# Layer 0's FFN of a two-layer encoder: background transfers issued by GpSimd, and layer 1's Fourier and recurrence input weights split there and loaded as pairs

## The chip, the cores and the metric

The kernel runs on one core of one Trainium2 chip. The metric is the device time of one execution in microseconds; the time of the kernel before is the median of three runs. One further execution was recorded by the hardware profiler, and all rows below come from it. The engines are PE (matrix products), DVE, ACT and POOL (GpSimd); SP only issues transfers here. Every engine works through its own instructions in order, and waits where one of them has to wait. A transfer issued by SP, ACT or POOL stands in that engine's order like any other instruction.

## The reference

Two layers, each with a mixing step and an FFN, on one sequence of 1024 positions and 1024 channels. Everything is float32.

```python
for l in range(DEPTH):
    mod = c_act @ w_ada[l] + b_ada[l]                  # 6 vectors of 1024: shift, scale, gate, twice
    sh1, sc1, gt1, sh2, sc2, gt2 = jnp.split(mod, N_MOD, axis=-1)
    h = modulate(rms_norm(x, g_mix[l]), sh1, sc1)
    p = h @ w_in[l]                                    # Fourier 256, recurrence 384, its gate 384, q, k, v
    y_f = fourier_mix(p_f, w_fourier[l])
    ...                                                # linear recurrence, neighbourhood attention
    y = jnp.concatenate([y_f, y_l, y_n], axis=-1) @ w_out[l]
    x = x + gt1[:, None, :] * y
    h = modulate(rms_norm(x, g_ffn[l]), sh2, sc2)
    f = (jax.nn.silu(h @ w_ffn_gate[l]) * (h @ w_ffn_up[l])) @ w_ffn_down[l]
    x = x + gt2[:, None, :] * f
return rms_norm(x, g_final)
```

## The kernel before

**Products in three parts.** PE multiplies rounded numbers. To come near float32, each operand is split into a rounded part, hi, and the rest, lo, and a product is three matmuls (hi hi, hi lo, lo hi). `split` makes the two: ACT rounds a raw tile into hi (line 199), DVE subtracts hi from it into lo (line 202). So a weight tile costs a load by SP, an ACT pass and a DVE pass before PE (line 191) can use it. In the traces the large tile of raw numbers is called plain, that of split numbers rounded, and U is 1024 columns, HALF 512.

**The FFN of a layer.** The hidden width is cut into slices f of 128. For every f seven P jobs of 12 matmuls each make the gate and up products of that slice (`P_ORDER`); their product is evacuated by ACT and DVE, split, and kept in a tile A: ffa_A for even f, ffb_A for odd f. Beside it lies the slice of down weights (ffa_DW, ffb_DW). In an even f the down products of the two slices before it are made: `down_pair` adds 12 matmuls and one DVE operation (line 205) at eight of the 14 hooks of that f (`PAIRS`). So the work repeats every two f's, 264 matmuls, and the down products of a pair can't start before the second half of its ffb_A is split. From f = 2 on this is one loop, in layer 0 from about 605 to 1185 us, in layer 1 from about 1702 to 2305.

**Background work in layer 0's FFN.** At each hook from f = 3 on, `bg` pulls one or two steps from a generator: first `half_steps`, the product of c with w_ada of layer 1, then `split_spill`. `half_steps` takes w_ada in 96 halves of 256 KB: SP loads one into a raw buffer (line 1527), and DVE multiplies it with c and adds up along the row, in one instruction, a matvec (line 1529), with a small one behind it that reads the sum. `split_spill` takes weights that layer 1 will want, 13 items in 26 pieces: SP loads a piece into the same raw buffer (line 255), ACT and DVE split it, SP stores hi and lo into a DRAM tensor, wspill (line 261). SP also loads the FFN's own weights (lines 1306 and 1457), in the order in which the code is written. There is one raw buffer and one buffer each for hi and lo (M0).

**Layer 1's start.** After the last P job of layer 0 come the last down products, the norm of layer 1 and the input projection, one tile of 128 columns a job. Its first nine loads (tiles T_F, T_F + 1, T_X, T_X + 1 for either half of the positions, then T_X + 2) go by `w_load`: SP loads, ACT and DVE split. The tiles from T_G on, the DFT matrices and wv go by `ready_load`: two loads of POOL's queue (lines 242 and 243) fetch hi and lo from wspill into one of three slots (WX: ready_WR and two slots of rounded). The squares of the norm at lines 380 and following run on ACT, DVE and POOL.

The core of what the change touches, as it stands before:

```python
for j in range(8):
    for i in range(2):
        self.nc.sync.dma_start(out=raw, in_=self.I["ada"][l, 8 * c + j, :, i * HALF:i * HALF + HALF])
        yield 1
        self.nc.vector.tensor_tensor_reduce(out=raw, in0=raw, in1=self.f(self.M0 + i * HALF, HALF), ...)
        yield 1
```

The order on ACT, DVE and PE in the FFN is that of the code: a hook issues its splits, its down pair and then its background steps.

## Time and profile before

| | us |
|---|---|
| median of three runs | 2347.38 (2344.06 to 2350.89) |
| the profiled execution | 2345.14 |
| its span in the trace | 2343.4 |
| PE busy | 2219.9 (95%) |
| DVE busy | 1750.5 (75%) |
| ACT busy | 964.2 (41%) |
| POOL busy | 377.8 (16%) |
| layer 0's FFN loop | about 605 to 1185 |
| layer 1's start | about 1185 to 1262 |
| layer 1's FFN loop | about 1702 to 2305 |

The span runs from the first to the last instruction in the trace; the execution is 1.74 us longer. A share of busy time is a mean over stages: PE is not short of work in the loops, so the places to look at are those where it stands, what it stands for, and what that waits for in turn. The granted clock of PE (PEclk) is given as a share of its full 2.4 GHz; 0.50 is the lower of its two levels, and a window that holds both has a value between. Line numbers are those of the kernel before; in the changed kernel the matvec is line 1532, its load 1528, the spill's load 251 and its store 255.

### The profile page before, as it was taken

Reading aid. Unit: us, or ns where it says so; the run is one execution under the profiler, and the core shown is the slowest. Engines: PE = TensorE matmul, PEld = TensorE weight load, DVE = VectorE, ACT = ScalarE, POOL = GpSimd, SP = SyncE. Lnnn points to the kernel's source line nnn. Section 1 sums busy time; section 2 is a strip of 40 time slices with the busy share of each in tenths; the row PEclk is TensorE's granted clock in tenths of the full one; section 3 lists DMA queues with packets and bytes.
Section 4 is the critical chain, followed back from the end, with each engine's and each line's share of the span. In section 5 each row is a group of like instructions: output and inputs, shape, how many; then the busy total and the mean of one; then the engine's idle time right before and its main releaser. Section 6 shows DMA issues by size and latency. Waiting matters only on the chain.

```text
span 2343.4 us, 27097 instructions
## 1 busy us (share of the span) xinstructions
PE 2219.9 (95%) x9802; PEld 1786.6 (76%) x9802; DVE 1750.5 (75%) x2840; ACT 964.2 (41%) x1608; POOL 377.8 (16%) x302
## 2 busy tenths in 40 slices
PE   6987998999999999999999999899999999999997
PEld 4765876778888887787777787678788888888886
DVE  8888689788788888776676456887876666666666
ACT  5365476444222222333244746745532222222223
POOL 4224276300000000000001445740000000000002
PEclk9997999989999999999999999999999999999998
DMA  8323423331333344465232262323021111111112
GB/s 299 103 67 111 133 82 121 109 118 46 102 121 115 121 124 121 135 201 171 66 133 76 69 195 69 106 80 113 28 63 54 55 54 54 55 52 48 55 37 77
DMA packets 91100, 230.53 MB, mean 98 GB/s; under 512 B 10451, under 2 KB 16083, under 8 KB 90966
## 3 DMA queue, kind: packets, MB, share of 16 engines
q1 hardware_dynamic: 82324, 194.42, 25.9%
q10 hardware_dynamic: 3746, 18.66, 2.3%
q0 software_dynamic: 4896, 15.73, 2.2%
q8 instruction: 77, 1.26, 0.2%
q14 instruction: 57, 0.47, 0.1%
HBM read 207.80 MB, written 20.97 MB: 98 GB/s over the span
## 4 chain that ended last, share of the span: by engine, by line
PE 64%; DVE 21%; DMA 7%; ACT 4%; issue 4%; POOL 1%; SPq 0%; ACTq 0%; DVEq 0%; POOLq 0%
PE psum L191 64%; DVE rounded L202 4%; DVE plain L202 3%; DMA plain<-in_ada 3%; DVE plain L205 2%; ACT plain L199 1%; DMA plain<-in_dft 1%; DVE plain L1529 1%; DVE psum L923 1%; DMA plain<-in_wv 1%; DVE psum L202 1%; DVE rounded L205 1%; DVE plain L341 1%; ACT lru_LF L199 1%; DVE lru_LF L725 1%
## 5 line engine op out<-in xcount | busy, mean ns | idle before, releaser
L191 PE MATMUL psum<-rounded 128*128 128x512 f32 (+2 forms) x4116 | 994.9, 391 | 20.8 <-DVE rounded L209 7.7
L191 PEld LDWEIGHTS psum<-rounded 128*128 128x128 f32 (+1 forms) x4116 | 771.5, 190 | 189.4 <-DVE rounded L209 11.5
L199 ACT ACTIVATE rounded<-plain 128x512 fp32r<-128x512 f32 (+4 forms) x404 | 263.8, 659 | 619.3 <-PE psum L191 472.1
L202 DVE TENSOR_TENSOR rounded<-plain,rounded 128x512 fp32r<-128x512 f32 (+4 forms) x410 | 317.8, 781 | 73.3 <-ACT rounded L199 70.1
L191 PE MATMUL psum<-hx_HX,rounded 128*128 128x512 f32 x1488 | 365.1, 392 | 1.9 <-DVE plain L202 1.9
L205 DVE SCALAR_TENSOR_TENSOR plain<-psum,plain 128x1024 f32<-128x1024 f32 (+2 forms) x256 | 269.9, 1062 | 111.5 <-PE psum L191 109.7
L191 PEld LDWEIGHTS psum<-hx_HX,rounded 128*128 128x128 f32 x1488 | 279.3, 188 | 63.9 <-ACT rounded L199 2.3
L191 PE MATMUL psum<-ffa_A,ffa_DW 128*128 128x512 f32 (+1 forms) x1080 | 299.8, 388 | 0.7 <-ACT plain L199 0.7
L191 PE MATMUL psum<-ffb_A,ffb_DW 128*128 128x512 f32 x960 | 275.0, 393 | 7.6 <-DVE ffb_A L202 4.3
L202 DVE TENSOR_TENSOR plain<-plain 128x512 f32<-128x512 f32 (+4 forms) x342 | 207.2, 617 | 73.1 <-DMA plain<-in_wu 41.2
L380 POOL TENSOR_TENSOR plain<-plain 128x512 f32<-128x512 f32 x6 | 8.1, 1357 | 1459.4 <-ACT plain L199 1459.4
L191 PEld LDWEIGHTS psum<-ffa_A,ffa_DW 128*128 128x128 f32 x1080 | 201.0, 188 | 43.9 <-ACT plain L199 1.5
L202 DVE TENSOR_TENSOR plain<-psum,plain 128x512 f32<-128x512 f32 (+1 forms) x288 | 193.4, 685 | 46.3 <-PE psum L191 42.5
L191 PEld LDWEIGHTS psum<-ffb_A,ffb_DW 128*128 128x128 f32 x960 | 179.7, 188 | 52.5 <-DVE ffb_A L202 8.6
L199 ACT ACTIVATE plain<-plain 128x512 f32<-128x512 f32 (+6 forms) x191 | 117.8, 629 | 152.2 <-DVE plain L202 76.7
L960 POOL TENSOR_TENSOR rounded<-qk_PE,rounded 128x512 fp32r<-128x512 f32 (+3 forms) x132 | 141.2, 1077 | 131.8 <-ACT rounded L199 107.6
L191 PE MATMUL psum<-rounded,v_V 128*65 128x512 f32 (+4 forms) x528 | 128.3, 357 | 14.5 <-ACT rounded L199 4.9
L191 PE MATMUL psum<-qk_QT 128*128 128x512 f32 (+8 forms) x432 | 107.7, 349 | 20.5 <-DVE plain L923 14.3
L191 PEld LDWEIGHTS psum<-rounded,v_V 128*65 128x65 f32 (+1 forms) x528 | 74.0, 149 | 52.2 <-POOL rounded L960 6.3
L202 DVE TENSOR_TENSOR psum<-psum,plain 128x256 f32<-128x256 f32 x240 | 97.7, 410 | 21.0 <-PE psum L191 14.3
L199 ACT ACTIVATE qk_PE<-psum 128x512 f32<-128x512 f32 (+4 forms) x168 | 83.4, 503 | 55.7 <-DVE psum L202 50.3
L199 ACT ACTIVATE ffa_DW<-plain 128x512 fp32r<-128x512 f32 x44 | 27.8, 631 | 186.0 <-PE psum L191 184.1
(140 smaller groups left out, 2138.2 us busy)
## 6 DMA issues: line engine op xcount, KB each, us to landing
plain<-in_ada SPq DMA_DIRECT2D x96, 256.0 KB, 2.6
plain<-in_wd SPq DMA_DIRECT2D x88, 256.0 KB, 2.6
plain<-in_wg SPq DMA_DIRECT2D x40, 512.0 KB, 3.6
plain<-in_wu SPq DMA_DIRECT2D x40, 512.0 KB, 3.6
plain<-in_ada SPq DMA_DIRECT2D x30, 512.0 KB, 3.5
wspill<-plain SPq DMA_DIRECT2D x44, 256.0 KB, 2.9
start_AT<-in_ada SPq DMA_DIRECT2D x18, 512.0 KB, 5.1
plain<-in_bias_t ACTq DMA_DIRECT2D x12, 768.0 KB, 4.6
```

The lines of the kernel that those rows point to most:

```text
L191: self.nc.tensor.matmul(out=out, lhsT=lhsT, rhs=rhs, start=start, stop=stop)
L199: self.nc.scalar.activation(out=out, in_=in_, func=func, **kw)
L202: self.nc.vector.tensor_tensor(out=out, in0=a, in1=b, op=op)
L205: self.nc.vector.scalar_tensor_tensor(out=out, in0=a, scalar=s, in1=b, op0=op0, op1=op1)
L341: self.nc.vector.tensor_tensor_reduce(out=raw, in0=raw, in1=self.f(self.M0, U), op0=ALU.mult, op1=ALU.add, scale=1.0, scalar=0.0, accum_ou ...
L380: (self.nc.gpsimd if eng[m] else self.nc.vector).tensor_tensor(out=accs[i], in0=accs[i], in1=ss[i], op=ALU.add)
L725: nc.vector.tensor_tensor_scan(out=t, data0=a, data1=i, initial=0.0, op0=ALU.mult, op1=ALU.add)
L923: self.nc.vector.tensor_tensor_reduce(out=s, in0=s, in1=self.f(bo, a * w).rearrange("p (a b) -> p a b", a=a), op0=ALU.add, op1=ALU.max, sc ...
L960: (self.nc.vector if PLAN[self.l]["lo"][self.step] else self.nc.gpsimd).tensor_tensor(out=pl, in0=p, in1=ph.bitcast(F32), op=ALU.subtract)
L1529: self.nc.vector.tensor_tensor_reduce(out=raw, in0=raw, in1=self.f(self.M0 + i * HALF, HALF), op0=ALU.mult, op1=ALU.add, scale=1.0, scalar ...
```

## The change

The loads of `half_steps` move from SP's queue to POOL's. They use two raw buffers in turn, the old one and `r2`, which is taken from the FFN's list of free temporaries (four stay in it instead of five). A step now issues the load of one half and the matvec of the half before: 97 steps instead of 192.

`split_spill` moves to POOL's queue as well. It loads into the two raw buffers in turn, splits the piece before, and stores hi and lo by one transfer out of one pair buffer in M0. A piece takes two steps instead of three. Five items come in (T_F, T_F + 1, T_X, T_X + 1, T_X + 2 of layer 1): 18 items, 36 pieces.

`ready_load` fetches hi and lo by one transfer of 1 MB instead of two of 512 KB; the slots (WX) are set at the last P job of layer 0's FFN, first two of rounded, later three. All jobs of layer 1's input projection take their weights this way. `bg` is called with one step at every hook. Steps in all: 171 instead of 270.

```diff
     def ready_load(self, i, n):
         def go():
-            hi, lo = [a[:, :n] for a in self.WX()]
-            self.nc.gpsimd.dma_start(out=hi, in_=self.ws[i, :, 0, :n])
-            self.nc.gpsimd.dma_start(out=lo, in_=self.ws[i, :, 1, :n])
-            return hi, lo
+            w = self.WX().rearrange("p (t n) -> p t n", t=2)[:, :, :n]
+            self.nc.gpsimd.dma_start(out=w, in_=self.ws[i, :, :, :n])
+            return w[:, 0], w[:, 1]
         return go
 
     def split_spill(self):
-        raw = self.f(10 * U + HALF, HALF)
-        for i, (w, n) in enumerate(src):
-            for c in range(0, n, HALF):
-                m = min(HALF, n - c)
-                self.nc.sync.dma_start(out=raw[:, :m], in_=w[:, c:c + m])
-                yield 1
-                hi, lo = [self.f(o, m).bitcast(F32R) for o in h]
-                self.split(raw[:, :m], hi, lo)
-                yield 1
-                for j, a in enumerate((hi, lo)):
-                    self.nc.sync.dma_start(out=self.ws[i, :, j, c:c + m], in_=a.bitcast(F32))
-                yield 1
+        q, h = self.nc.gpsimd, self.f(self.M0, U).bitcast(F32R).rearrange("p (t n) -> p t n", t=2)
+        pieces = [(i, w, c, min(HALF, n - c)) for i, (w, n) in enumerate(self.spilled()) for c in range(0, n, HALF)]
+        for j, (i, w, c, m) in enumerate(pieces + [(0, None, 0, 0)]):
+            if w is not None:
+                q.dma_start(out=self.raw2(j)[:, :m], in_=w[:, c:c + m])
+            if j:
+                i, w, c, m = pieces[j - 1]
+                self.split(self.raw2(j - 1)[:, :m], h[:, 0, :m], h[:, 1, :m])
+                q.dma_start(out=self.ws[i, :, :, c:c + m], in_=h[:, :, :m].bitcast(F32))
+            yield 1
+            yield 1
...
+    SPILL = (T_G, T_G + 1, T_G + 2, T_K, T_Q, T_F, T_F + 1, T_X, T_X + 1, T_X + 2)
...
+    def raw2(self, j):
+        return self.f((10 * U + HALF, self.r2)[j % 2], HALF)
...
-        i = {T_G: 0, T_G + 1: 1, T_G + 2: 2, T_K: 3, T_Q: 4}.get(t) if l else None
-        if i is not None:
-            return self.ready_load(i, U), fn, True
+        if l:
+            return self.ready_load(self.SPILL.index(t), U), fn, True
...
-            self.WX = Ring([slot(self.WR1, 0), slot(self.RA, 16 * U), slot(self.RA, 18 * U)])
+            self.WX = Ring([self.WR1, *self.WX.items[::-1]])
...
             if l == 0 and f == FIRST + 1 and i == 0:
+                self.r2 = self.free.pop()
...
-            self.bg(1 if f % 2 or i < 3 or i > 10 else 2)
+            self.bg(1)
 
     def half_steps(self, seq):
+        halves = [(l, c, j, i) for l, c in seq for j in range(8) for i in range(2)]
+        for q, (l, c, j, i) in enumerate(halves + [(0, 0, 0, 0)]):
+            if q < len(halves):
+                self.nc.gpsimd.dma_start(out=self.raw2(q), in_=self.I["ada"][l, 8 * c + j, :, i * HALF:i * HALF + HALF])
+            if q:
+                l, c, j, i = halves[q - 1]
+                part, raw = [self.mod[l] + 8 * c, self.tiny], self.raw2(q - 1)
+                self.nc.vector.tensor_tensor_reduce(
...
+            yield 1
...
                 self.WH, self.WS = Ring([o, 34 * U - o]), U
+                self.WX = Ring([self.RA[:, a:a + 2 * U] for a in (o, 34 * U - o)])
```

**The order on DVE.** First the middle of layer 0's FFN, at the down weights of the second pair of f's. The rows named ISA are the matvec (128x512) and the reading of its sum (128x1); a wait named DMAHW is on a transfer of SP's or ACT's queue, DMASW on one of POOL's. Before:

```order
L202 TENSOR_TENSOR rounded<-plain,rounded 128x512 [waits PE_49,Activation_49]
L205 SCALAR_TENSOR_TENSOR plain<-plain 128x8 [waits DVE_49]
L202 TENSOR_TENSOR plain<-psum,plain 128x512 [waits PE_49]
L1529 ISA plain<-plain 128x512 [waits DMAHW0_49]
L1529 ISA plain 128x1
L202 TENSOR_TENSOR plain<-psum,plain 128x512 [waits DVE_49]
L202 TENSOR_TENSOR rounded<-plain,rounded 128x512 [waits Activation_49]
```

After, on DVE at the same down weights:

```order
L1532 ISA plain<-plain 128x512 [waits DMASW2_49]
L1532 ISA plain 128x1
L1532 ISA plain<-plain 128x512 [waits DMASW3_49]
L1532 ISA plain 128x1
L202 TENSOR_TENSOR plain<-psum,plain 128x512 [waits PE_49]
L202 TENSOR_TENSOR rounded<-plain,rounded 128x512 [waits DMAHW2_49,Activation_49]
L202 TENSOR_TENSOR plain<-plain 128x512 [waits DMAHW3_49]
L205 SCALAR_TENSOR_TENSOR plain<-psum,plain 128x1024 [waits PE_49]
L1532 ISA plain<-plain 128x512 [waits DMASW4_49]
```

One matvec between some six other operations has become two side by side, every four or so.

**The order on ACT.** The end of a pair of f's during the spill, where the two halves of ffb_A are rounded. A row plain<-plain that waits for a DMA is the rounding of a piece of the spill into M0. Before, on ACT:

```order
L199 ACTIVATE plain<-plain 128x512 [waits DMAHW5_49,DMAHW3_49,Activation_49]
L199 ACTIVATE rounded<-plain 128x512 [waits DVE_49,PE_49]
L199 ACTIVATE plain<-plain 128x512 [waits DVE_49]
L199 ACTIVATE plain<-plain 128x512 [waits DMAHW7_49,DMAHW1_49,Activation_49]
L199 ACTIVATE rounded<-plain 128x512 [waits DVE_49,PE_49]
L199 ACTIVATE rounded<-plain 128x512 [waits PE_49]
L199 ACTIVATE ffb_A_3674<-plain 128x512 [waits DVE_49]
```

After, on ACT at the end of a pair of f's, each spill rounding waiting for its own load and for the store of the piece before:

```order
L199 ACTIVATE plain<-plain 128x256 [waits DMASW2_49,DMASW1_49,Activation_49]
L199 ACTIVATE plain<-plain 128x512 [waits DVE_49]
L199 ACTIVATE rounded<-plain 128x512 [waits DVE_49,PE_49]
L199 ACTIVATE ffb_A_3674<-plain 128x512 [waits DVE_49]
L199 ACTIVATE plain<-plain 128x512 [waits DMASW4_49,DMASW3_49,Activation_49]
L199 ACTIVATE rounded<-plain 128x512 [waits PE_49]
L199 ACTIVATE rounded<-plain 128x512 [waits DMAHW1_49,PE_49]
L199 ACTIVATE ffb_A_3674<-plain 128x512 [waits DVE_49]
```

A rounding of the spill now stands between the two halves of ffb_A as well, and its two waits are both for POOL's transfers.

**The order on POOL.** The change of layers: squares of layer 1's norm (plain<-plain) and the loads from wspill. Before:

```order
L380 TENSOR_TENSOR plain<-plain 128x512 [waits DMAHW2_49,DMAHW1_49,DMAHW3_49,PE_49,DMAHW5_49,Activation_49,Pool_49]
L380 TENSOR_TENSOR plain<-plain 128x512 [waits Activation_49] x2
L242 DMA ready_WR_8026<-wspill 128x1024 [waits DMAHW2_49,DMAHW6_49,DVE_49,PE_49]
L243 DMA ready_WR_8026<-wspill 128x1024 [waits DMAHW7_49,DMAHW4_49]
L242 DMA rounded<-wspill 128x1024 [waits DMAHW1_49,DMAHW5_49,DVE_49,PE_49]
L243 DMA rounded<-wspill 128x1024 [waits DMAHW6_49,DMAHW2_49,PE_49]
```

After, on POOL, from the last stores of the spill on:

```order
L255 DMA wspill<-plain 256x1x512 [waits DMASW6_49,DVE_49]
L255 DMA wspill<-plain 256x1x256 [waits DVE_49]
L242 DMA rounded<-wspill 128x2048 [waits DMASW0_49,DVE_49,PE_49]
L242 DMA rounded<-wspill 128x2048 [waits DVE_49,PE_49]
L384 TENSOR_TENSOR plain<-plain 128x512 [waits DMASW5_49,Activation_49,Pool_49]
L384 TENSOR_TENSOR plain<-plain 128x512 [waits Activation_49] x2
L242 DMA ready_WR_8022<-wspill 128x2048 [waits DMASW2_49,DVE_49,PE_49]
```

Two loads of whole pairs have moved ahead of the squares, and each load from wspill is one row where there were two.

## Rows read from the trace of the kernel before

**Rows 1.** The page, part 1: busy us, share of the span, instructions.

```profile
PE 2219.9 (95%) x9802; PEld 1786.6 (76%) x9802; DVE 1750.5 (75%) x2840; ACT 964.2 (41%) x1608; POOL 377.8 (16%) x302
```

**Rows 2.** The chain that ended last, by time: start us, us, what.

```profile
610.24 0.70 DVE plain L1529 x2
...
619.01 2.40 DVE plain L202 x4
626.90 30.06 PE psum L191 x130
...
687.91 30.03 PE psum L191 x130
...
854.52 0.71 DVE plain L1529 x2
855.24 2.63 DMA plain<-in_ada
...
870.97 30.03 PE psum L191 x130
...
995.18 30.02 PE psum L191 x130
...
1034.10 0.70 DVE plain L202
1035.20 3.94 DMA plain<-in_dft
...
1121.90 62.02 PE psum L191 x263
...
1701.05 602.59 PE psum L191 x2633
```

**Rows 3.** Waits of PE, 605 to 1185: us in total, times, longest.

```profile
PE psum L191 <- DVE ffb_A L202: 3.3, 7, 0.7
PE psum L191 <- ACT ffb_A L199: 3.2, 3, 2.2
```

**Rows 4.** Busy time by window: us, PE, PEld, DVE, ACT, POOL, granted clock, DMA share, GB/s.

```profile
1120.76:1124.20 3.44, 2.79 (x7) 2.02 (x8) 1.69 (x3) 0.61 (x1) 0.00 (x0) 0.71 0.47 157
...
1216.27:1219.70 3.43, 3.43 (x18) 3.14 (x19) 0.87 (x2) 0.27 (x1) 0.00 (x0) 0.72 0.47 158
```

**Rows 5.** PE's timeline after 1121.90: start us, us, engine, line, operation, tiles, count.

```profile
1122.70 1.48 PE L191 MATMUL psum<-ffa_A,ffa_DW 128*128 128x512 f32 x3
...
1126.81 0.85 PE L191 MATMUL psum<-ffa_A,ffa_DW 128*128 128x512 f32 x3
```

**Rows 6.** Line 1529, the matvec: ns min/median/max; idle of DVE ahead of it (us, times).

```profile
L1529 DVE CUSTOM_DVE_ANT_0 plain<-plain x96: 677/684/696, 610.2 to 972.9; 128x512 f32<-128x512 f32 x96
...
  DMA plain<-in_ada: 26.5, 37
```

**Rows 7.** DMA issues on SP: count, KB each, median us from issue to landing.

```profile
plain<-in_ada SPq DMA_DIRECT2D x96, 256.0 KB, 2.6
...
plain<-in_wg SPq DMA_DIRECT2D x40, 512.0 KB, 3.6
...
xspill<-plain SPq DMA_DIRECT2D x8, 512.0 KB, 2.9
```

**Rows 8.** Line 242, POOL's load of hi from wspill (512 or 384 KB).

```profile
DMA to landing us min/median/max: 3.9/4.3/5.3
```

**Rows 9.** Line 255, SP's loads of the spill's pieces.

```profile
DMA to landing us min/median/max: 2.6/3.7/4.7
```

**Rows 10.** PE's timeline at layer 1's start.

```profile
1216.27 1.82 PE L191 MATMUL psum<-plain 128*128 128x1 f32 x14 [1.28 <-DVE plain L380]
```

**Rows 11.** DVE's timeline there.

```profile
1214.38 1.23 DVE L202 TENSOR_TENSOR rounded<-plain,rounded 128x1024 fp32r<-128x1024 f32 x1 [0.43 <-ACT rounded L199]
```

**Rows 12.** Line 243, POOL's load of lo, issued behind that of hi.

```profile
DMA to landing us min/median/max: 4.2/4.9/7.2
```

**Rows 13.** POOL's timeline: the first load into rounded.

```profile
1258.10 0.53 POOL L242 DMA_DIRECT2D rounded<-wspill  x1 [53.67 <-PE psum L191]
```

More of the change, by code (lines that the diff above doesn't have):

```diff
@@ L137, in __init__ @@
         self.xs = dr.tile([8, P, S], F32, name="xspill")
-        self.ws = dr.tile([13, P, 2, U], F32, name="wspill")
+        self.ws = dr.tile([18, P, 2, U], F32, name="wspill")
         self.X0 = 0
@@ L240, in go, with spilled @@
         def go():
[L241 to L244 removed]
+            w = self.WX().rearrange("p (t n) -> p t n", t=2)[:, :, :n]
+            self.nc.gpsimd.dma_start(out=w, in_=self.ws[i, :, :, :n])
+            return w[:, 0], w[:, 1]
         return go
     def split_spill(self):
[L248 to L262 removed]
+        q, h = self.nc.gpsimd, self.f(self.M0, U).bitcast(F32R).rearrange("p (t n) -> p t n", t=2)
[10 more added lines that the diff above has]
+    SPILL = (T_G, T_G + 1, T_G + 2, T_K, T_Q, T_F, T_F + 1, T_X, T_X + 1, T_X + 2)
+    def spilled(self):
+        src = [(self.I["w_in"][1, t], U) for t in self.SPILL]
+        return src + [(self.I["dft"][c], U) for c in range(4)] + [(self.I["wv"][1, k], 768) for k in range(4)]
+    def raw2(self, j):
+        return self.f((10 * U + HALF, self.r2)[j % 2], HALF)
     def pull(self):
@@ L1087, in mix @@
             wx = self.open("ready", WR1=(2 * U, F32R))
-            slot = lambda a, o: (a[:, o:o + U], a[:, o + U:o + 2 * U])
-            self.WX = Ring([slot(self.WR1, 0), slot(self.RA, 16 * U), slot(self.RA, 18 * U)])
+            self.WX = Ring([self.WR1, *self.WX.items[::-1]])
             self.deep = 2
@@ L1518, in hook @@
                 self.c_spread()
-            self.bg(1 if f % 2 or i < 3 or i > 10 else 2)
+            self.bg(1)
     def half_steps(self, seq):
-        raw = self.f(10 * U + HALF, HALF)
-        for l, c in seq:
-            part = [self.mod[l] + 8 * c, self.tiny]
-            for j in range(8):
-                for i in range(2):
-                    self.nc.sync.dma_start(out=raw, in_=self.I["ada"][l, 8 * c + j, :, i * HALF:i * HALF + HALF])
-                    yield 1
-                    self.nc.vector.tensor_tensor_reduce(
-                        out=raw, in0=raw, in1=self.f(self.M0 + i * HALF, HALF), op0=ALU.mult, op1=ALU.add,
-                        scale=1.0, scalar=0.0, accum_out=self.f(part[i] + j, 1))
-                    yield 1
-            m = self.f(part[0], 8)
-            self.tt(m, m, self.v(l, V_ADA + 8 * c, 8), ALU.add)
-            self.tt(m, m, self.f(self.tiny, 8), ALU.add)
+        halves = [(l, c, j, i) for l, c in seq for j in range(8) for i in range(2)]
[6 more added lines that the diff above has]
+                self.nc.vector.tensor_tensor_reduce(
+                    out=raw, in0=raw, in1=self.f(self.M0 + i * HALF, HALF), op0=ALU.mult, op1=ALU.add,
+                    scale=1.0, scalar=0.0, accum_out=self.f(part[i] + j, 1))
+                if (j, i) == (7, 1):
+                    m = self.f(part[0], 8)
+                    self.tt(m, m, self.v(l, V_ADA + 8 * c, 8), ALU.add)
+                    self.tt(m, m, self.f(self.tiny, 8), ALU.add)
+            yield 1
     def ffn_jobs(self, l):
```

7 lines of the change are left out of this document (2 added, 5 removed).

## The prediction

> **What bounds the kernel now.** The page's first part comes first: TensorE (PE) is busy 95% of the span, DVE 75%, ACT 41% [rows 1], so the question is where PE is not. The chain of waits [rows 2] shows where. Layer 1's FFN is one unbroken piece of PE work, 2633 matmuls in 602.59 us, 0.229 us a matmul. In layer 0's FFN the same work is broken at even distances: a pair of f's is 264 matmuls, 60.42 us at that rate, and the pieces begin later and later against it. From 626.90 to 870.97 lie four pairs, 244.07 us against 241.68: 2.4 lost. From 870.97 to 1121.90 lie four more, 250.93 us: 9.25 lost. Between the pieces the chain names matvecs and in_ada loads in the first stretch, in_dft and other loads of the spill in the second. PE's table of waits for the stage [rows 3] has the end of it: 6.5 us in ten waits for ffb_A tiles. After the longest of them the granted clock is 0.71 [rows 4]; three matmuls there take 1.48 us, three at full clock 0.85 [rows 5]. Eight ran so, at about 0.43 instead of 0.23: 1.6 us. So this FFN holds 2.4 + 9.25 + 1.6 = **13.3 us** that can be won, and none of it is PE's own work.
>
> Why ffb_A is late is read off DVE. It works in order, and each of the 96 matvecs (0.684 us, [rows 6]) stands in its row between the splits that PE needs. 37 times DVE idled until an in_ada load landed, 26.5 us in all. Load and matvec share one buffer: a load is issued when the matvec before it ends, and DVE stands until it has landed. The spill has the same form, a chain of load, ACT rounding, DVE subtraction, next load. 22 of its 26 loads are issued between 995.18 and 1121.90 [rows 2]: 126.72/22 = 5.76 us each, 11 a pair, 63.4 us where PE wants 60.42. That is the 3 us a pair that the second stretch loses.
>
> **The change, part by part.** (1) *ada halves on GpSimd's queue, two buffers.* The matvecs now stand in pairs (first order excerpt), 28 to a pair of f's. The work is the same 96; what decides is the cycle of the two buffers, from one pair of matvecs to the next: c = 0.71 + 0.01 + L + 0.03, the first two from the matvec at 854.52 and the load issued behind it at 855.24 [rows 2], the last an allowance for the semaphore. L, a 256 KB load issued by GpSimd, is in no row. On SP that load lands in 2.6, one of 512 KB in 3.6 [rows 7]; on GpSimd 512 KB takes 4.3 [rows 8]. So the ends are 2.6 and 4.3, and I take 2.6 + (4.3 - 3.6) = **3.3**, GpSimd's surcharge at equal size added to SP's row of the same size, the nearest. c = 4.05.
>
> A pair of matvecs can't start before the first, at 610.24 [rows 2], plus its cycles. By the new order 10 matvecs stand ahead of the second ffb_A of the first pair of f's, 41 ahead of the next one, 69 and 96 ahead of the others. First: 610.2 + 4c + 3.7 (a matvec and five operations of 0.60 behind it, as in the four at 619.01) = 630.1, against 626.90: 3.2 late. Second: 610.2 + 20c + 1.9 = 693.1 against 687.91 [rows 2]: **5.2** late. Third: 610.2 + 34c + 1.9 = 749.8, before the 753.5 that PE reaches a pair after the second, so nothing is added. Twenty cycles make it steep: L = 3.1 gives 1.2, 3.65 gives 12, 2.6 nothing, and L = 4.3 (c = 5.05) holds every later pair of f's to 14c = 70.7, some 43 over the stage.
>
> The Trainium skill, page "DMA: Bandwidth & Descriptors", section "Anatomy of one DMA — SWDGE (gpsimd) path", gives a fixed 2.0 us and the bytes at 436 GB/s for such a transfer: an estimate of 2.6 for 256 KB, 3.2 for 512 KB. The row of 512 KB has 4.3 [rows 8], so the trace speaks against that price; by the page's figure the ada halves would cost PE nothing. Its section "Issuing engine by pattern" names Sync for plain loads, which speaks against this move.
>
> (2) *The spill.* 18 items in 36 pieces instead of 13 in 26, on GpSimd, loads double-buffered, but one buffer for hi and lo. The chain is now ACT rounding, DVE subtraction, store's landing, next rounding: the rounding waits for the store before it (second excerpt), and ACT, in order, holds the ffb_A rounding behind it. Before, 5.76 less the load's 3.7 [rows 9] leaves 2.06 for ACT, DVE and what lies between; 0.4 of it is the two stores' own issue ahead of the next load (1034.10 + 0.70 to 1035.20, [rows 2]). So a cycle is 1.66 + L. L, a 512 KB store by GpSimd: at least 2.9, SP's xspill store of that size [rows 7], at most 4.3 [rows 8]; I take 2.9 + 0.7 = 3.6, by the same surcharge. A cycle is 5.26. ACT's new order holds 10 pieces in the first pair of f's, 12 in each of the next two: 12 x 5.26 = 63.1, 2.7 over, twice, of which ACT's look-ahead over PE hides a little: **4**. It decides from 60.42/12 = 5.03. At L = 2.9 it costs nothing; at 4.3 it is 12 x 5.96 = 71.5, 11.1 over, 22 in all. The ten added pieces' roundings and subtractions are hidden: ACT and DVE have the room [rows 1].
>
> (3) *SP loses 96 ada loads and the spill.* Weight loads no longer queue behind an SP that waits for a matvec: part of the 13.3, nothing on top. One step a hook instead of one or two: 171 steps instead of 270, which end in time either way. If they did not, the rest would stand in the open ahead of the last down projections.
>
> (4) *Layer 1's start.* The w_in tiles of Fourier and recurrence inputs come split: nine SP loads, nine ACT roundings and nine DVE subtractions go. On the path stands one: PE waited 1.28 at 1216.27 [rows 10] for DVE, which had a subtraction of 1.23 at 1214.38 just ahead [rows 11]; then the granted clock is 0.72 [rows 4], another 1.6. Removed: 2.9; late next is the square itself, which then ends about when PE comes. Added: one load of 1 MB in place of two of 512 KB. The second landed 4.9 after its issue [rows 12], issued behind the first one's 0.53 [rows 13]: about 5.5. A half job is 24 matmuls, 24 x 0.229 = 5.5. Where a single slot turns over, the load just fills the job, so I put 0.5, from 0 to +4 if each of five such jobs waits 0.8. Sum **-2.4** (-2.9 to +1.1). The squares on GpSimd stand behind two of these loads (third excerpt); those wait for a slot that the last P jobs no longer read, so they cost two issues of 0.53 before the squares' inputs exist.
>
> **Sum.** -13.3 + 5.2 + 4 + 1.5 (a few waits like those of [rows 3] that stay) - 2.4 = -5.0 on a span of 2343.4: 2338.4, and 1.74 around it (2345.14 profiled): 2340.1. The profiled execution lies 2.24 under the median 2347.38, so the median should be **2342**.
>
> **Rivals.** *A, the forecast*: 2342, 0.42. *B, GpSimd's transfers are as quick as SP's*: neither cycle reaches PE, -13.3 + 1.5 - 2.4 = -14.2, 2333. For it: GpSimd's engine has nothing else to do in this stage, and the 4.3 was measured with two loads in flight. Against: that row lies 0.7 over SP's. 0.25. The page's price named above points the same way. *C, the store's landing paces ACT*: the single hi/lo buffer makes each rounding wait for it; at 4.3 two pairs of f's take 71.5, 18 more than in A, +13.0: 2360, slower. It passes the time before from a cycle of 5.5. For it: the second of two GpSimd transfers took 4.9 [rows 12]. Against: SP's stores land sooner than its loads of that size [rows 7]. 0.18. *D, the ada loads pace DVE at 4.3*: +43 instead of +5.2: 2380; it needs a half-size load to take what a full one does. 0.07. *E, it doesn't do what it says*: ffb_A is late by DVE's order, not by the transfers, and only layer 1's start is won: 2345. DVE's 26.5 us idle for the loads [rows 6] and the chain's DMAs [rows 2] speak against. 0.08.
>
> **Numbers.** A measurement tells about 0.3%, 7 us, from no change: faster is under 2340.3, slower over 2354.4. A lies at 2335 to 2349 by its bounds: 0.14 under, 0.27 within, 0.01 above. B: 0.24 faster, 0.01 within. C: 0.16 slower, 0.02 within. D: slower. E: within. Together 0.38, 0.38, 0.24. The range of 8 in 10 takes A, B, E and the lower half of C: 2331 to 2361.
>
> **What would show it.** Loads of in_ada by GpSimd landing in 3.1 to 3.5; two matvecs every 4.05 in the first pair of f's; PE waiting for ffb_A some 3 us near 630 and 2 more near 690, then hardly until the spill; stores of wspill landing near 3.6 with ACT idle until they do, and pairs of 61 to 63 us from 930 on; no split ahead of PE near 1216. B shows as PE work that runs on from pair to pair; C as ACT's table of waits led by wspill stores. The forecast falls if the loads land outside 2.9 to 3.7, or if the spill's cycle passes 5.5.

## The result, and the profile after

| | before | after |
|---|---|---|
| median, us | 2348.56 (4 runs) | 2379.78 (2377.9 to 2382.98, 4 runs) |
| profiled execution / span, us | 2345.14 / 2343.4 | 2382.98 / 2381.1 |

The changed kernel is 1.4% slower: the ratio is 1.0138, with a 95% interval from 1.0121 to 1.0155. The forecast was 2342 in a range from 2331 to 2361, so it has the wrong sign and the time is outside the range.

Both programs have the same 9802 matmuls in the same order, so they can be laid side by side: how much later does the same matmul run? Each column below is the start in one trace less the start in the trace of before, read at nine places (the other columns belong to the experiments below, the last row is the difference of the spans).

| before at, us | after | e5 | r3 | r2 | r1 | r4 | e7 | e9 |
|---|---|---|---|---|---|---|---|---|
| 610 | 2.4 | -2.7 | 1.7 | 2.7 | 0.2 | 0.9 | 0.7 | -3.6 |
| 671 | 10.0 | -1.4 | 5.7 | 5.2 | 8.3 | 1.3 | 0.2 | 5.8 |
| 731 | 22.7 | 8.1 | 10.6 | 10.7 | 8.8 | 3.6 | 1.8 | 17.2 |
| 791 | 29.2 | 14.8 | 15.4 | 11.4 | 10.0 | 3.8 | 2.6 | 23.7 |
| 852 | 34.8 | 22.5 | 21.4 | 15.1 | 10.3 | 5.2 | 4.2 | 31.3 |
| 942 | 34.7 | 39.0 | 24.4 | 16.2 | 12.1 | 5.4 | 3.8 | 52.0 |
| 1002 | 40.5 | 45.5 | 24.3 | 21.7 | 10.3 | 3.6 | 2.0 | 50.7 |
| 1183 | 33.0 | 44.6 | 16.8 | 14.2 | 2.8 | -3.2 | -5.5 | 43.2 |
| 1303 | 35.1 | 46.2 | 18.2 | 15.8 | 4.2 | -4.4 | -5.8 | 44.8 |
| span | 37.7 | 50.0 | 19.7 | 18.5 | 9.4 | -3.4 | -0.6 | 48.0 |

After loses 32.4 us between 610 and 852, where the ada halves are worked off, and 5.7 more up to 1002, in the spill. Then 7.5 come back, since before still spills there and loses and after has finished. Layer 1's start gives +2, not -2.4. (The first row differs by several us either way among kernels whose code up to there is the same; so a few us here are the scatter of one execution. The last row adds 2.6 to 3.1 us to the value at 2305 in every column but r3's, in code that is the same: the end of before's one execution was quick.)

After's first part of the page answers to [rows 1]: busy us, share, instructions. PE's busy time has grown by 17 us for the same matmuls, which is the slower clock behind waits.

```profile
PE 2237.1 (94%) x9802; PEld 1798.3 (76%) x9802; DVE 1750.6 (74%) x2841; ACT 960.4 (40%) x1609; POOL 469.6 (20%) x462
```

After's table of PE waits, 605 to 1185 us (total, times, longest), answers to [rows 3]:

```profile
PE psum L191 <- ACT ffb_A L199: 17.1, 6, 5.2
PE psum L191 <- DVE ffb_A L202: 3.6, 6, 1.1
PE psum L191 <- ACT rounded L199: 3.4, 2, 1.9
PE psum L191 <- DVE plain L202: 2.1, 2, 1.8
```

The tile that PE waits for is the same, ffb_A, but 20.7 us instead of 6.5. The first matmuls on it in each pair of f's, from after's timeline of PE (start us, us; idle before and its releaser in brackets), answer to the pieces of [rows 2]:

```profile
634.60 0.79 PE L191 MATMUL psum<-ffb_A,ffb_DW 128*128 128x512 f32 x1 [5.19 <-ACT ffb_A L199]
635.75 0.80 PE L191 MATMUL psum<-ffb_A,ffb_DW 128*128 128x512 f32 x1 [0.35 <-DVE ffb_A L202]
...
708.25 1.22 PE L191 MATMUL psum<-ffb_A,ffb_DW 128*128 128x512 f32 x2 [0.71 <-DVE ffb_A L202]
...
775.79 0.79 PE L191 MATMUL psum<-ffb_A,ffb_DW 128*128 128x512 f32 x1 [0.54 <-DVE ffb_A L202]
...
843.45 0.79 PE L191 MATMUL psum<-ffb_A,ffb_DW 128*128 128x512 f32 x1 [1.10 <-DVE ffb_A L202]
...
967.64 0.73 PE L191 MATMUL psum<-ffb_A,ffb_DW 128*128 128x512 f32 x2 [0.23 <-DVE ffb_A L202]
...
1034.10 1.08 PE L191 MATMUL psum<-ffb_A,ffb_DW 128*128 128x512 f32 x2 [0.65 <-DVE ffb_A L202]
```

The pairs take 72.5, 67.5 and 67.7 us while matvecs run, then 124.2 for two and 66.5 while the spill runs, where PE's own work is 60.42.

Now DVE. The matvec's line in after (idle of DVE ahead of it until what; then who waited for the matvec: us, times) answers to [rows 6], its load's line to [rows 8]:

```profile
  DMA plain<-in_ada: 28.2, 46
...
  POOL plain L1528: 174.7, 87
```

```profile
L1528 POOL DMA_DIRECT2D plain<-in_ada x96: 537/537/735, 570.7 to 838.5; - x96
...
DMA to landing us min/median/max: 2.7/2.9/5.5
```

The loads land sooner than I had put them, in 2.9 instead of 3.3. But they start later. DVE's and POOL's timelines in after, one turn of one buffer:

```profile
624.03 0.69 DVE L1532 CUSTOM_DVE_ANT_0 plain<-plain 128x512 f32<-128x512 f32 x1 [0.24 <-DMA plain<-in_ada]
624.65 0.08 DVE L1532 DVE_READ_ACCUMULATOR2_ANT plain<- 128x1 f32 x1
...
628.13 0.69 DVE L1532 CUSTOM_DVE_ANT_0 plain<-plain 128x512 f32<-128x512 f32 x1 [0.31 <-DMA plain<-in_ada]
```

```profile
625.14 0.55 POOL L1528 DMA_DIRECT2D plain<-in_ada  x1 [0.40 <-DVE plain L1532]
```

The matvec ends at 624.73, POOL's issue starts at 625.14: 0.41 us, where SP starts 0.03 after it in before (0.01 in the chain, [rows 2]). This turn is 4.10 us, near the shortest (3.9). As a floor my cycle of 4.05 was right in sum, from two wrong terms. It isn't what set the time, though: 28 matvecs a pair would then take 57 us. Of the 94 turns of a buffer in after, from the start of one matvec on it to the next, 35 last under 4.25 us; the others are longer, up to 6.9, and the mean is 4.8. In 34 of the longer ones the matvec had no wait at all: DVE's other work filled the turn.

The window over the 96 matvecs, before and then after (us; PE, PEld, DVE, ACT, POOL busy; granted clock, DMA share, GB/s):

```profile
610.20:973.60 363.40, 360.94 (x1570) 293.95 (x1570) 298.21 (x540) 100.28 (x169) 0.00 (x0) 1.00 0.39 119
```

```profile
614.20:842.10 227.90, 207.36 (x857) 165.98 (x855) 190.23 (x390) 56.82 (x95) 51.29 (x95) 0.95 0.48 154
```

After puts the same matvecs into 228 us instead of 363. The 228 us hold 857 matmuls, 3.25 pairs of f's, for which PE needs 196 at full clock. DVE is busy 190 of it, 58.6 a pair, and 37.7 idle, 28.2 of that for the loads. So its work alone nearly fills the 60.4 us of a pair, and the 11.6 us of idle a pair come on top. (That busy and idle fill the window is so by definition; what each is worth in time is for the experiments to show.)

### The profile page after: what moved, and what is told of

The parts are those of the page before. It is cut to its first block, busy times and chain, and to the rows that moved or that the text cites. A ratio compares the mean times of both kernels' runs of the same rounds, so it can differ in the third digit from the quotient of the medians.

```text
span 2381.1 us, 27062 instructions
## 1 busy us (share of the span) xinstructions
PE 2237.1 (94%) x9802; PEld 1798.3 (76%) x9802; DVE 1750.6 (74%) x2841; ACT 960.4 (40%) x1609; POOL 469.6 (20%) x462
## 4 chain that ended last, share of the span: by engine, by line
PE 56%; DVE 18%; issue 12%; DMA 7%; ACT 3%; POOL 3%; SPq 0%; POOLq 0%; ACTq 0%; DVEq 0%
PE psum L191 56%; DVE rounded L202 3%; DMA wspill<-plain 3%; DVE plain L202 2%; POOL plain L1528 2%; DVE plain L205 2%; ACT plain L199 1%; DVE plain L345 1%; DMA plain<-in_ada 1%; DVE psum L926 1%; DVE start_AT L345 1%; DVE psum L202 1%; ACT lru_LF L199 1%; DVE lru_LF L728 1%; ACT rounded L199 1%
## 5 line engine op out<-in xcount | busy, mean ns | idle before, releaser
L191 PE MATMUL psum<-rounded 128*128 128x512 f32 (+2 forms) x4116 | 999.0, 393 | 22.7 <-DVE rounded L209 7.2
L191 PEld LDWEIGHTS psum<-rounded 128*128 128x128 f32 (+1 forms) x4116 | 774.6, 191 | 193.2 <-DVE rounded L209 10.7
L199 ACT ACTIVATE rounded<-plain 128x512 fp32r<-128x512 f32 (+4 forms) x395 | 254.0, 649 | 584.4 <-PE psum L191 441.0
L202 DVE TENSOR_TENSOR rounded<-plain,rounded 128x512 fp32r<-128x512 f32 (+4 forms) x401 | 307.6, 773 | 60.2 <-ACT rounded L199 56.8
L202 DVE TENSOR_TENSOR plain<-plain 128x512 f32<-128x512 f32 (+5 forms) x352 | 216.4, 626 | 69.3 <-ACT plain L199 38.3
L191 PEld LDWEIGHTS psum<-ffb_A,ffb_DW 128*128 128x128 f32 x960 | 182.6, 191 | 67.4 <-ACT ffb_A L199 19.7
L202 DVE TENSOR_TENSOR plain<-psum,plain 128x512 f32<-128x512 f32 (+1 forms) x288 | 193.6, 685 | 44.6 <-PE psum L191 40.7
L199 ACT ACTIVATE plain<-plain 128x512 f32<-128x512 f32 (+6 forms) x201 | 123.9, 629 | 190.8 <-DVE plain L202 78.2
L1528 POOL DMA_DIRECT2D plain<-in_ada x96 | 52.0, 542 | 329.2 <-DVE plain L1532 174.7
L199 ACT ACTIVATE plain<-psum 128x512 f32<-128x512 f32 (+1 forms) x119 | 69.1, 587 | 100.0 <-PE psum L191 99.9
```

The source lines that it names most:

```text
L191: self.nc.tensor.matmul(out=out, lhsT=lhsT, rhs=rhs, start=start, stop=stop)
L199: self.nc.scalar.activation(out=out, in_=in_, func=func, **kw)
L202: self.nc.vector.tensor_tensor(out=out, in0=a, in1=b, op=op)
L1528: self.nc.gpsimd.dma_start(out=self.raw2(q), in_=self.I["ada"][l, 8 * c + j, :, i * HALF:i * HALF + HALF])
```

## The experiments

Two explanations of the loss stood against each other, and both are at odds with the forecast. *Queue* (theory Q in the expectations): GpSimd issues later and lands later than SP, DVE executes in order, and so stands for the difference. *Rate* (theory D or R): 28 matvecs a pair instead of 16 overfill DVE, whoever loads.

How many matvecs and spill pieces stand ahead of the second ffb_A of each pair of f's, counted in the order of the built programs, belongs to all of this. The background steps in the code don't fix these numbers alone: the build puts ACT's and DVE's instructions of this stage in an order of its own, which the sentence on the code's order ahead of the diff left out. So r3 and e9, whose edits touch neither hooks nor steps, have a somewhat different order from after.

| | matvecs ahead of it, DVE | a pair | pieces a pair, ACT |
|---|---|---|---|
| before, e5 | 5, 21, 37, 53, 69, 85, 96 | 16 | 11 to 12 |
| after, r2 | 10, 41 (r2: 40), 69, 96 | 28 | 12 |
| r3 | 9, 41, 69, 96 | 28 to 32 | 12 |
| e9 | as after | 28 | 14 to 15 |
| r1 | 10, 31, 53, 75, 96 | 22 | 10 to 11 |
| r4, e8 | 6, 28, 50, 72, 94, 96 | 22 | 10 |
| e6, e7, e12 | 6, 29, 52, 75, 96 | 23 | 10 to 11 |
| e10, e11 | 4, 27, 50, 73, 96 | 23 | 10 |

**e5: the queue alone.** The kernel before, one edit.

```diff
-                    self.nc.sync.dma_start(out=raw, in_=self.I["ada"][l, 8 * c + j, :, i * HALF:i * HALF + HALF])
+                    self.nc.gpsimd.dma_start(out=raw, in_=self.I["ada"][l, 8 * c + j, :, i * HALF:i * HALF + HALF])
```

> The kernel before with one edit: the 96 loads of w_ada's halves are issued by GpSimd instead of SP; one buffer, the old steps and the old rate. Theory Q (the queue's later issue and landing is what DVE stands for): each matvec's data comes 0.4 + 0.3 = 0.7 us later, 16 or so to a pair of f's, 11 us a pair, of which DVE's free time takes about 7: 3 to 4 us a pair over six pairs, about 2365 (+12 to +25). Theory R (the rate of background steps alone did it, the queue is cheap): within 4 us of before, 2349 to 2353.

Measured: 2397.16 (2395.15 to 2402.77), ratio 1.0209 (1.0187 to 1.0231), 49 us slower than before. The queue alone costs more than the whole change does. DVE's idle ahead of the matvec, and the window over the 96 matvecs, in e5:

```profile
  DMA plain<-in_ada: 83.2, 66
```

```profile
607.80:1017.70 409.90, 380.52 (x1590) 305.22 (x1589) 301.16 (x540) 99.78 (x169) 51.21 (x95) 0.96 0.34 106
```

Against before, DVE's work is the same (301 and 298 us), its idle for the loads grows from 26.5 to 83.2, +57, and the window grows from 363.4 to 409.9, +46.5. A load comes (0.41 - 0.03) + (2.9 - 2.6) = 0.68 us later, 96 of them 65 us: nearly all of it becomes DVE idle, and four fifths of that becomes time. Both expectations were too small; I had let DVE's free time take 7 of 11 us a pair. What DVE waited for can be read in before, in DVE's table of waits from 605 to 973 us (total, times, longest):

```profile
DVE plain L1529 <- DMA plain<-in_ada: 26.5, 37, 2.0
DVE plain L202 <- DMA plain<-in_wu: 13.7, 10, 2.0
DVE ffa_DW L202 <- ACT ffa_DW L199: 8.3, 6, 1.7
DVE plain L202 <- PE psum L191: 7.2, 8, 1.4
DVE rounded L202 <- ACT rounded L199: 6.8, 7, 2.1
DVE plain L205 <- PE psum L191: 2.9, 4, 1.0
```

and in e5, from 605 to 1030:

```profile
DVE plain L205 <- PE psum L191: 14.2, 15, 2.2
DVE plain L202 <- DMA plain<-in_wu: 6.8, 6, 2.4
```

DVE is idle for 65.2 us in before's window and 108.7 in e5's. Without the waits for in_ada that is 38.7 and 25.5: the 13 us that the other waits gave up are what the 57 did not cost in time (DVE's work, 3 us more, makes up the 46.5). It is tempting to say that DVE's free time was its 10 us of waiting for PE (7.2 + 2.9), but the trace of e5 speaks against it: those waits grew to 14.2. What did shrink is the wait for in_wu, 13.7 to 6.8, and that for ACT's ffa_DW, of which none is left; for in_wu the likely reason, which no run tests, is that SP no longer holds those loads behind ada loads that wait for a matvec.

DVE's and POOL's timelines in e5 show that the late issue isn't contention with DVE:

```profile
639.86 0.69 DVE L1529 CUSTOM_DVE_ANT_0 plain<-plain 128x512 f32<-128x512 f32 x1 [0.94 <-DMA plain<-in_ada]
640.47 0.08 DVE L1529 DVE_READ_ACCUMULATOR2_ANT plain<- 128x1 f32 x1
642.11 0.69 DVE L202 TENSOR_TENSOR plain<-plain 128x512 f32<-128x512 f32 x1 [1.55 <-DMA plain<-in_wu]
...
645.12 0.08 DVE L1529 DVE_READ_ACCUMULATOR2_ANT plain<- 128x1 f32 x1
645.12 0.68 DVE L202 TENSOR_TENSOR plain<-psum,plain 128x512 f32<-128x512 f32 x1
```

```profile
640.96 0.54 POOL L1527 DMA_DIRECT2D plain<-in_ada  x1 [3.50 <-DVE plain L1529]
645.61 0.55 POOL L1527 DMA_DIRECT2D plain<-in_ada  x1 [4.11 <-DVE plain L1529]
```

POOL starts 0.41 us after the matvec's end both times, once with DVE idle behind it (640.55 to 642.11), once with DVE busy.

**r2: the changed kernel with SP's queue for the ada loads.**

```diff
-                self.nc.gpsimd.dma_start(out=self.raw2(q), in_=self.I["ada"][l, 8 * c + j, :, i * HALF:i * HALF + HALF])
+                self.nc.sync.dma_start(out=self.raw2(q), in_=self.I["ada"][l, 8 * c + j, :, i * HALF:i * HALF + HALF])
```

> The changed kernel with the loads of w_ada's halves back on SP's queue, two buffers and one step a hook kept; only the issuing engine differs. Theory Q: the cycle of two matvecs shortens by 0.36 of issue and 0.3 of landing, 14 cycles a pair, so the pairs near 67 to 72 us return to about 61 and the time to about 2350 or below. Theory D: the 28 us in which DVE stood for these loads shrink by about half at most, and its work still fills the odd f's: 2365 to 2372.

Measured: 2358.66 (2356.91 to 2363.69), ratio 1.0053 (1.0034 to 1.0071): 21 us of the 31 are gone, between what the two expected. DVE's idle ahead of the matvec and the window of the 96 in r2:

```profile
  DMA plain<-in_ada: 7.6, 15
```

```profile
612.90:820.90 208.00, 201.81 (x863) 163.48 (x862) 188.49 (x390) 56.60 (x94) 0.74 (x1) 0.98 0.54 168
```

DVE's idle falls from 37.7 to 19.5 and the window by 19.9. What is left (12.4 us up to 852 in the table) is for the smaller part the loads, 7.6 us of waiting: DVE is busy 91% there.

**r3: half the work in each matvec, the queue as in after.**

```diff
-                    out=raw, in0=raw, in1=self.f(self.M0 + i * HALF, HALF), op0=ALU.mult, op1=ALU.add,
+                    out=raw[:, :256], in0=raw[:, :256], in1=self.f(self.M0 + i * HALF, 256), op0=ALU.mult, op1=ALU.add,
```

> The changed kernel, but each matvec multiplies only 256 of the 512 columns that were loaded, so half of c times w_ada of layer 1 is left out; loads, queues, rate and order stay. It takes about 0.27 us from each of the 96 matvecs, 7.5 us a pair, 26 in all. Theory D: nearly all of that returns, about 2355. Theory Q: the cycle of the two buffers is load latency and hardly shorter, so at most 14 x 0.27 = 3.8 a pair, 2367 or more.

Measured: 2368.21 (2364.97 to 2375.2), ratio 1.0097 (1.007 to 1.0125). The matvec, its idle and the window in r3:

```profile
L1532 DVE CUSTOM_DVE_ANT_0 plain<-plain x96: 409/424/428, 612.5 to 823.9; 128x256 f32<-128x256 f32 x96
...
  DMA plain<-in_ada: 42.1, 47
```

```profile
612.50:824.30 211.80, 199.12 (x850) 159.59 (x849) 161.98 (x384) 52.91 (x90) 51.29 (x95) 0.99 0.51 164
```

28 us of DVE work are gone (190.2 to 162.0), and 12 come back as idle (37.7 to 49.8). The time saved is 11.6 of the 26 that the rate's theory wanted; the queue's theory (2367 or more) had it right. DVE's work is 50 us a pair here, no more than in before (298 us in 5.95 pairs), and r3 still loses 19.7 us on before from 610 to 852. So a DVE that is filled by its own work isn't needed for a loss: the changed kernel's loads on GpSimd's queue, in its order, are enough.

**r1 and r4: fewer steps a pair, queue as in after.** r1 takes a step at two hooks of three; r4 takes as many, but mostly in even f's.

```diff
-            self.bg(1)
+            self.bg(int((14 * f + i) % 3 != 2))          # r1
+            self.bg(int(f % 2 == 0 or i % 3 == 0))       # r4
```

> The changed kernel with a background step at two of three hooks instead of every hook: 18.7 matvecs and 9.3 spill pieces to a pair of f's instead of 28 and 12 to 14; nothing else differs. Theory D (DVE is overfilled by the rate of background steps: 38 us of its own work a pair and 28 matvecs of 0.61 make 55, and the stalls on loads come on top in series): the layer 0 FFN loses its 24 us from 627 to 1184 and more, 2380 goes to about 2342. Theory Q (the GpSimd queue's later issue, 0.4 us, and landing, 2.9 us, pace the two buffers): fewer cycles a pair also help, 9.3 x 4.8 = 45 of 60 us, so it too expects under 2350; this run tells the size of what the rate costs, not which of the two it is. If neither, and the loss is contention of GpSimd's descriptor work with DVE or DMA traffic, the time stays over 2370.

> The changed kernel with a background step at every hook of an even f and at every third hook of an odd f: 19 to a pair, as many as in the two-thirds run, but placed in the even f's, which last 41 us for PE against 19 for an odd one. Theory D in its sharper form (it is the odd f that is overfilled: 14.4 us of DVE's own work and 14 matvecs of 0.61 make 23 where PE takes 19, and ffb_A is due right behind it): faster than the two-thirds run by 2 to 6 us, about 2338. If only the mean rate counts, within 2 us of the two-thirds run. Theory Q: the same as the two-thirds run, or slower, since the loads come closer together in the even f's.

Measured: r1 2354.37 (2347.59 to 2359.77, 10 runs), ratio 1.0022 (1.0007 to 1.0038); r4 2344.95 (2335.68 to 2351.8, 10 runs), ratio 0.9985 (0.9967 to 1.0002). So the rate is worth 25 us and the place another 9, with everything still on GpSimd's queue. Contention of GpSimd's issuing with other traffic, r1's third possibility, would have kept the time over 2370. PE's waits, 605 to 1230, in r4:

```profile
PE psum L191 <- DVE ffb_A L202: 3.6, 6, 0.6
PE psum L191 <- DVE rounded L205: 2.9, 8, 0.4
PE psum L191 <- ACT ffb_A L199: 2.2, 2, 1.6
```

and in r1, where one wait of 4.5 us opens at the first pair (table, 671):

```profile
PE psum L191 <- ACT ffb_A L199: 6.4, 3, 4.5
```

The place was expected to matter in every odd f. The table says otherwise: r1 loses 8.1 us at the first pair, where 10 matvecs stand ahead of its ffb_A as in after, and r4 0.4, with 6; from 671 on they run alike (2.0 and 3.9 up to 852, and both gain 7 to 8 in the spill). So what the place bought is the first pair, where the matvecs begin late, behind the load of c, and the first ffb_A is due at once. An overfilled odd f in the later pairs is not shown.

**e6 and e7: r4 with SP's queue, for the ada loads and then for the spill as well.**

```diff
+            self.bg(int(f % 2 == 0 or i % 3 == 0))
+                self.nc.sync.dma_start(out=self.raw2(q), ...)       # e6, e7: ada
+        q, h = self.nc.sync, ...                                    # e7: the spill's loads and stores
```

> The changed kernel with steps at every hook of even f's and every third of odd ones (as the even-f run) and the loads of w_ada's halves on SP's queue. Theory Q: the 4 us that the even-f run still lost up to 850 us go too, 2338 to 2342 against its 2345. Theory R: no different from the even-f run, 2345, or a little slower, since SP's queue holds weight loads behind waits for matvecs again.

> As the run before, and the spill's loads and stores on SP's queue as well; only the loads from wspill in layer 1 stay on GpSimd. If GpSimd's queue also costs in the spill (its stores land 0.3 later and are issued 0.4 later), 0 to 2 us faster than with the spill on GpSimd. If at this rate the spill's cycle is hidden anyway (9 pieces a pair, 5.3 us each, 48 of 60), the same within 1.5 us, or slower if FFN weight loads queue behind the spill on SP.

Measured: e6 2342.97 (12 runs), ratio 0.999 (0.9973 to 1.0008); e7 2340.78 (12 runs), 0.9967 (0.9952 to 0.9981). e6 can't be told from r4. e7 is faster than before by its interval, though not clearly than r4. At this rate and place the queue is worth 0 to 4 us, against 49 in e5. And from every hook to r4's place the ada loads on SP's queue gain 16 us (r2 to e6), those on GpSimd's 35 (after to r4): queue and rate both cost, and each costs more where the other is bad.

**e9: the spill's pair stored by two transfers again.** It was to show that the store's landing paces the spill.

```diff
-                q.dma_start(out=self.ws[i, :, :, c:c + m], in_=h[:, :, :m].bitcast(F32))
+                for t in range(2):
+                    q.dma_start(out=self.ws[i, :, t, c:c + m], in_=h[:, t, :m].bitcast(F32))
```

> The changed kernel, but hi and lo of a spilled piece are stored by two transfers of 256 KB, as before, on GpSimd's queue, so that the next rounding waits for the store of hi alone and the next subtraction for that of lo. If the landing of the pair store paces the spill (5.3 us a piece now, ACT waiting 75 us for stores): hi's store leaves before the subtraction, the cycle falls by about 0.7 to 1 us to 4.3 to 4.6, 12 pieces stay under 60 us a pair, and the 9 us that the stretch from 843 to 1034 us loses shrink: 2371 to 2375. If that stretch loses by its DVE work or by the queue's issue time (two issues of 0.6 instead of one of 0.69), 2378 to 2383.

Measured: 2392.42 (2383.4 to 2397.33), ratio 1.0172 (1.0145 to 1.0198), 13 slower than after: neither expectation. The cycle did fall: the spill's 36 loads span 169.2 us (832.0 to 1001.2) against 190.6 in after (836.9 to 1027.5), 4.83 us a piece instead of 5.45. But the edit changed the build's order too: a pair of f's now holds 14 to 15 pieces instead of 12. 15 x 4.83 = 72.5, and PE's timeline in e9 has these pairs:

```profile
838.50 1.22 PE L191 MATMUL psum<-ffb_A,ffb_DW 128*128 128x512 f32 x2 [0.81 <-DVE ffb_A L202]
...
910.46 1.22 PE L191 MATMUL psum<-ffb_A,ffb_DW 128*128 128x512 f32 x2 [0.35 <-DVE ffb_A L202]
...
983.01 1.22 PE L191 MATMUL psum<-ffb_A,ffb_DW 128*128 128x512 f32 x2 [0.69 <-DVE ffb_A L202]
```

72.0 and 72.6 us, for 14 and 15 pieces. In after 12 x 5.45 = 65.4 stands against a last spill pair of 66.5 us. So pieces a pair times the cycle fits the second pair of e9 and the last of after; the first of e9 (14 x 4.83 = 67.6) is 4 us longer than that. It is weak evidence in any case, since the mean cycle is taken from the same stretch as the time. What the run does say is that its time alone would have misled: the cycle fell, and more pieces a pair took more than it gave. The way the pieces stall has changed as well: DVE's first wait in e9, 833 to 1005 us, is for the second store.

```profile
DVE plain L202 <- DMA wspill<-plain: 27.0, 20, 2.5
```

**e8, e10, e11, e12: layer 1's part, and a later place.** e8 is r4 without the part at layer 1's start (13 items spilled, the nine jobs by `w_load`). e10 is e7 with the steps behind the ffb_A split, e11 is e10 without layer 1's part, e12 is e7 without it.

```diff
+            self.bg((i > 2) + (2 < i < 11) if f % 2 == 0 else int(i == 0))       # e10, e11
-    SPILL = (T_G, T_G + 1, T_G + 2, T_K, T_Q, T_F, T_F + 1, T_X, T_X + 1, T_X + 2)
+    SPILL = (T_G, T_G + 1, T_G + 2, T_K, T_Q)                                    # e8, e11, e12
-        if l:
+        if l and t in self.SPILL:                                                # e8, e11, e12
```

> The even-f run (everything on GpSimd) without the part of the change at layer 1's start: 13 items are spilled instead of 18, and the nine jobs of Fourier and recurrence inputs load and split their weights themselves as in the kernel before; the other loads stay pairs of 1 MB. If that part is worth the 2.4 us of the forecast, this is 2 to 3 us slower than the even-f run (2347); if the waits for 1 MB loads in the single jobs eat it up, the same, 2345; under 2343 if they cost more than the splits did.

> The changed kernel with the background transfers of layer 0's FFN on SP's queue and the steps placed behind the ffb_A split: none at hooks 0 to 2 of an even f, two at hooks 3 to 10, one at hooks 11 to 13, one at the first hook of an odd f; 20 to a pair. If what still loses some 3 us up to 850 us in the even-f run on SP is background work ahead of ffb_A, 2 to 4 us faster than that run's 2341: 2337 to 2339. If two steps at one hook let DVE stand on the second's load (2.6 us with only one other operation between), that comes back as PE waits in the even f's and it is slower, 2342 to 2350.

> As the run before, without the part of the change at layer 1's start (13 items spilled, the nine jobs split their weights themselves). If that part is worth the forecast's 2.4 us, 2 to 3 us slower than the run before; if it is worth nothing, as the even-f pair of runs says, within 1.5 us of it.

> What is left of the change when the parts that the runs found costly or worthless are taken out: two raw buffers, one pair buffer and one step of load and matvec, but on SP's queue, at every hook of even f's and every third of odd ones, with 13 items spilled and the nine jobs of layer 1's start splitting their own weights; the loads from wspill stay pairs of 1 MB. If layer 1's part costs the 2 to 3 us by which both pairs of runs were faster without it, about 2338 where the kernel before has 2348 (ratio 0.996 or less). If those differences were scatter, the same as the even-f run on SP: ratio 0.997.

| | us | ratio | 95% |
|---|---|---|---|
| r4, with layer 1's part | 2344.95 | 0.9985 | 0.9967 to 1.0002 |
| e8, without | 2342.2 | 0.9972 | 0.9962 to 0.9982 |
| e10, with | 2345.35 | 0.9982 | 0.997 to 0.9994 |
| e11, without | 2343.69 | 0.9975 | 0.9964 to 0.9986 |
| e7, with | 2340.78 | 0.9967 | 0.9952 to 0.9981 |
| e12, without | 2341.77 | 0.997 | 0.9959 to 0.9981 |

Three pairs, -2.7, -1.7 and +1.0: layer 1's part is worth nothing that can be told here. e12's expected 0.996 did not come; it was 0.997, as expected if those differences were scatter. The later place of e10 isn't better than e7's, perhaps worse. The best versions, e7, e12 and e8, lie about 0.3% under before, and 1.6% under the changed kernel.

## Why the prediction was wrong

**What bounds the kernel: right.** PE waits for ffb_A, and ffb_A is late by DVE's order and its loads. That holds in after and most of the runs; in e5 and r3 PE waits for other tiles of DVE's as well.

**Part 1, the sentence that failed: "The work is the same 96; what decides is the cycle of the two buffers".** I took the chain of loads as a lower bound on time, 20 cycles of 4.05, compared it with PE's clock, and called the result the lateness: the term +5.2. The short turns take 3.9 to 4.2, so the price was fine; the mean turn is 4.8. DVE does not do its other work inside the cycle for free. It does it in order: a turn with more work than 4.1 us lasts as long as the work, one with less waits for the load, and the long ones don't make up for the short ones. I had forecast 3.2 us late, then 2.0 more (5.2 in all), then nothing, against a stretch in which before itself loses 2.4. It was 7.6 over before by 671, 12.7 more by 731, then 6.5 and 5.6: 32.4 in place of about 3. The sum to make was what DVE is asked for in a pair: 50 us in before, 12 or 13 matvecs more at 0.61 make 58, and that leaves 2 of 60.4 for every wait. I never made it; "ACT and DVE have the room", said of the spill, took the mean of the whole span for this stage. r3 shows that work taken out partly turns into idle, e5 that idle put in turns into time, r2 that idle taken out comes back as time. The two signs by which the forecast was to fall didn't show (loads at 2.9, the lower bound; the spill's cycle at 5.45, under 5.5), because both watch transfers and neither DVE's work.

**The terms of c.** L was 2.9 and not 3.3, and the time from matvec to issue was 0.41 and not 0.01, a term for which I used SP's row without a bound. That GpSimd's wait to issue could differ from SP's did not occur to me; together they are 0.68 us a load. The Trainium skill, page "DMA: Bandwidth & Descriptors", section "Specifications", puts the first byte at about 1 us for GpSimd's path and 0.6 for SP's: the 0.3 in landing is near the 0.4 between them; of the 0.38 ahead of the issue the section says nothing. The estimate of 2.6 us by the Trainium skill, same page, section "Anatomy of one DMA — SWDGE (gpsimd) path", which I had named, was 0.3 too low for 256 KB, in the direction the trace of before had already said.

**"28 to a pair" was in the text and not priced.** The rate rises from 16 to 28 matvecs and I wrote that 171 steps "end in time either way". They end too early: the changed kernel is done with them at 1036 us, with 180 us of the loop unused. r1 and r4 show 25 and 35 us for spreading them, r4's with fewer ahead of the first ffb_A.

**Part 2, the spill: the wait was as drawn, the size a little low.** The store lands in 3.2 (forecast 3.6), but is issued 0.4 later; the cycle is 5.45 (forecast 5.26), ACT waits 75 us for stores as drawn, and the stretch from 843.45 to 1034.10 takes 190.65 against 181.26: 9.4 lost, where I had 4 and a share of the 1.5. After's lines of the store and of ACT's wait:

```profile
DMA to landing us min/median/max: 2.5/3.2/5.8
```

```profile
ACT plain L199 <- DMA wspill<-plain: 74.8, 28, 5.5
```

The store's landing does pace the spill: of the 34 roundings that can be set beside a store in after's trace, 32 start within 0.15 us of its landing. The rule "pieces a pair times the cycle against 60.42" is less sure. In r4, where 10 x 5.45 stays under it, nothing is lost against before (table, 852 to 1183); but in after, from first matmul on ffb_A to the next, two pairs with 12 pieces each took 61.7 and 66.0 us.

**Part 4, layer 1's start: a small gain, given back.** PE's timeline in after, answering to [rows 10], POOL's timeline at a single job, and its loads' landing:

```profile
1250.04 1.72 PE L191 MATMUL psum<-plain 128*128 128x1 f32 x14 [0.45 <-DVE plain L384]
...
1292.81 3.69 PE L191 MATMUL psum<-rounded 128*128 128x512 f32 x15 [0.76 <-ACT plain L199]
```

```profile
1264.34 0.53 POOL L242 DMA_DIRECT2D rounded<-wspill  x1 [5.81 <-PE psum L191]
```

```profile
DMA to landing us min/median/max: 4.7/5.1/6.8
```

The wait of 1.28 is 0.45. But the slow clock behind it stayed (0.79 from 1250 to 1258 in after, 0.79 from 1216 to 1224 in before), so 1.6 of my 2.9 did not come. From there to the matmul that before starts at 1303, after loses 1.3 us more than before did. I would have put that to the single jobs, with a load of 5.1 behind POOL's wait for the slot; but in after's trace nothing up to 1300 waits for such a load, and PE's one wait there is the 0.76 for ACT. What took the gain back is not shown. In three pairs of runs nothing is left of the part.

**The rivals.** Rival D's number, 2380, is what came, and by chance: it needed loads of 4.3 us, and they took 2.9. C and D had the sign, but no rival had the mechanism: all of them kept DVE's own work out of the sum.

**What stays open.** Why GpSimd takes 0.41 us from semaphore to issue; only that DVE's activity doesn't set it. Whether e7's 2 to 4 us over r4 are the queue or scatter. What the build's order would be for a given number of steps a pair: it was read off after the fact, and e9's 15 pieces were not foreseen. Which part of DVE's idle time can take up a later load without cost. And what it costs that `r2` takes one of five free temporaries: no run puts it back; e7 and e12, which also do without it, are not slower than before, but at 28 matvecs a pair it was not separated.

## What to carry to other kernels

Before a transfer is moved to another queue, ask who stands for it in order: an in-order engine's work and its stalls add up, and idle time on it is no cover as such. DVE had 65 idle us in this stretch, and still 96 times 0.68 us, 65 in all, became 49 us of time. Background steps that are made cheaper must not run faster for that: spread them over the whole stretch that can hide them, with few ahead of the first tile that is due. And count them in the order of the built program, not in the code.
